# Four units of a projection sum in PSUM banks borrowed from the scan, and three weights' low parts move from POOL to VectorE

## The chip, the cores and the metric

The kernel runs on one core of one Trainium2 chip. The metric is the device time of one execution, in microseconds (us); the number given for a kernel is the median of its runs.

## The reference

One inference step of a two-layer encoder for 1024 new frames and 64 frames of a running stream, 1088 columns in all. Layer 0 mixes with a Mamba-2 scan (SSD), layer 1 with attention over a band of chunks; a gated feed-forward part follows each. The change lies in the entry of layer 0's mixer:

```python
zxbcdt = u @ w_in                       # u: rmsnorm of x, (1088, 1024)
z   = zxbcdt[..., :D_INNER]             # 2048 columns
xbc = zxbcdt[..., D_INNER:D_INNER + CONV_DIM]
dt_raw = zxbcdt[..., D_INNER + CONV_DIM:]
conv = conv_b
for k in range(CONV_W):                 # 4 taps
    conv = conv + padded[:, k:k + L] * conv_w[k]
xbc = silu(conv)                        # -> x (2048), B (4 x 128), C (4 x 128)
dt = softplus(dt_raw + dt_bias)
Acs = cumsum(dt * A)                    # within each chunk
y = scan(x, dt, Acs, B, C, state)       # decays exp(Acs_i - Acs_j), states from chunk to chunk
y = (y + x * D) * silu(z)
```

All arithmetic is float32. A matmul is made of three passes: each operand is split into a high part (rounded to the form that TensorE takes, float32r) and a low part (the rest), and high x high, high x low and low x high are summed.

## The kernel before, in words

Everything is held transposed, features on the 128 partitions and frames along the free axis, in three **slices** of 384, 384 and 320 columns (`SL`). The output features of `w_in` are taken in tiles of 128: x0 to x15, z0 to z15, four tiles each of B and C. A **unit** is one tile of one slice: 8 blocks of the contraction, 3 matmuls each, 24 in all (L417 to L419), summed in one PSUM bank, then evicted. Half a unit is 12 matmuls; after it the emitter may put other PE work in between (`st.pump()`).

**PSUM.** Eight banks: the pool `mm` has two (units), `ax` two (transposes and small products), `yy` four. `yy` serves three things one after the other: the entry's first units (tile `mmp`) and the products for dt (`dtp`); then the three transposed tables of Acs (`acT`, L683); then, for the rest of the mixer, the scan's outputs `yp` and `yo` (L864, L873). A pool hands its banks out in turn, and the next user of a bank waits for the last reader of the one before.

**Weights.** One tile of weights is loaded into `raw` (two buffers), then split by `part`: ACT casts the high part (L301) and another engine subtracts for the low part (L302) into `hl` (three buffers). That engine is `W.eng` where it is set, VectorE (DVE) otherwise. `W.eng` is POOL from just ahead of the entry's first units until the last of its nine, and in this stretch three weights are split: those of x1, z0 and x2, as B0's, C0's and x0's weights come free. Nothing else on POOL there is longer than 0.42 us.

**The entry.** First come B0, C0 and x0, three slices each. Then pairs follow by the list `order`; the first pair is x1 and z0, in the sequence x1 slice 0, z0 slice 0, x1 slice 1, z0 slice 1, x1 slice 2, z0 slice 2. Each x, B or C unit is evicted by DVE (L698, times the norm's factor; in two pieces for the third slice) into `craw` (three buffers), then convolved: ACT makes the first tap (L736) into `cvt` (a single buffer), DVE adds three (L738), ACT applies silu (L742, L744, L745) into the tile named by its kind: `BT`, `CT`, `xsT`. POOL copies the three halo columns between slices (L721, L726, L729). A z unit is evicted into `zs`.

Between these units PE also makes, for each slice of B0 and C0, the transposes `bnp` of BT (L762) and the products `cbp` of CT and BT (L768); and the table of dt is made: DVE steps L652 to L666 (a softplus by a series), products `acsp` (L669) and `lastp` (L674), the transposes `acT` (L683), DVE and ACT copies of them to `acr` (L684, L686), DMAs to DRAM (L685, L687), and from there the broadcast rows `dm` (L789) with which the scan's masks begin (L821, L825, L826). `dec` and `cd` (L688 to L690) are two further tables.

PE's order is that of the program text; the order on the other engines is set by the scheduler of the tile framework, from priorities and its own estimates.

Of the kernel before, what the change touches and what calls it, by code (L numbers as in the profile page):

```python
# [8 lines left out]
F32 = mybir.dt.float32  # L9
# [7 lines left out]
P = 128  # L17
# [6 lines left out]
SL = [(0, 384), (384, 384), (768, 320)]  # L24
# [14 lines left out]

GAP_A, GAP_B = 1.8, 1.2  # L40
HNP = 400
RB_WAIT = 4.8
CHW = ((13.1, 8.8, 18.0), (7.5, 6.0, 20.5)), ((9.0, 5.2, 18.0), (10.5, 8.0, 21.0))
AT_W1, AT_W2 = 6.0, 2.5
# [291 lines left out]
def hybrid_kernel(  # L336
# [5 lines left out]
    V, A, G, PE = nc.vector, nc.scalar, nc.gpsimd, nc.tensor  # L342
# [24 lines left out]
    for _ in range(17):  # L367
# [14 lines left out]
    W = Weights(  # L382
        nc, Ring(wp, "raw", RAWB, [P, 1024]), Ring(wp, "hl", HLB, [P, 2, 1024], F32R),
        Ring(None, "half", 0, [P, 2, 512], F32R), Ring(None, "tt", 0, [P, 1024]),
    )
# [16 lines left out]
    def mm(name):  # L402
        return pmm.tile([P, 512], F32, tag="mm", name=name)
# [5 lines left out]
    def passes(ps, w, rhs, ks, n, parts=2, first=True, last=True):  # L409

        h, v = w["w"]
        nk = len(ks)
        cut = (nk + parts - 1) // parts
        for i, (kw, k) in enumerate(ks):
            h_, l_ = h[:, kw * P:(kw + 1) * P], v[:, kw * P:(kw + 1) * P]
            xh, xl = rhs(k)
            PE.matmul(ps[:, :n], h_, xh, start=(first and i == 0), stop=False)  # L417
            PE.matmul(ps[:, :n], h_, xl, start=False, stop=False)  # L418
            PE.matmul(ps[:, :n], l_, xh, start=False, stop=(last and i == nk - 1))  # L419
            st.t += 3 * n / MMR  # L420
            if (i + 1) % cut == 0 and i + 1 < nk:
                st.pump()

    def unit(w, u, n, evac, parts=2, pl=None):
        ps_ = mm("mm") if pl is None else pl.tile([P, 512], F32, tag="mm", name="mmx")
        passes(ps_, w, lambda k: u[k], [(k, k) for k in range(KD)], n, parts=parts)
        evac(ps_)
        st.pump()
# [40 lines left out]
    def diag(r3, nb):  # L469
        dg = DG.get()  # L470
        V.tensor_tensor(
            dg[:, :nb], ident.unsqueeze(1).to_broadcast([P, nb, P]), r3.unsqueeze(2).to_broadcast([P, nb, P]), op=ALU.mult
        )
        return dg
# [11 lines left out]
    def rb_steps(ssum, n, out, wait=None, rb=None, more=None):  # L486
# [5 lines left out]
        with tc.high_priority(HIP):  # L492
            dg = diag(nr[:, :nb], nb)
        yield 0.1, wait or RB_WAIT
        with tc.high_priority(HIP):
# [15 lines left out]
    u, ucells = {}, {}  # L511
# [11 lines left out]
    order = []  # L523
# [47 lines left out]
    def project(qs, uq, y, src, after=None, early=None, pl=None):  # L571
# [3 lines left out]
        for mg in MGS:  # L575
            ws = early if early and mg is MGS[0] else [W.get() for _ in mg]
            for q in qs:
                n = QS[q][1]
                st.wait_for(lambda: q in uq)
                for m, w_ in zip(mg, ws):  # L580
                    ym = y[q][m // 4][:, m % 4, :]

                    def ev(ps):
                        with tc.high_priority(HIP):
                            if src is None:
                                A.copy(ym, ps[:, :n])
                            else:
                                V.tensor_tensor(ym, src[q][m // 4][:, m % 4, :], ps[:, :n], op=ALU.add)

                    if not (ws is early and q == qs[0]):  # L590
                        unit(w_, uq[q], n, ev, pl=pl)
                    if after:
                        if m == 0:
                            ss[q] = ssum_start(n)
                        add_sq(ss[q], ym, n, m == 0)
                    if q == qs[-1]:
                        W.put()
                if mg is MGS[-1]:
                    R.put(4)
                    if src is not None and src is not y:  # L600
                        R.put(2)
                    if after:
                        after(q, ss[q])

    with ExitStack() as es:
        pyy = es.enter_context(tc.tile_pool(reuse_waits="tile", name="pyy", bufs=4, space=PSUM))
# [172 lines left out]
        def ssd_task(j, s):  # L779
# [55 lines left out]
            for i in range(3):  # L835
# [5 lines left out]
                hn = sb2.tile([P, P], F32, tag="h", bufs=6, name="hn")  # L841
                with tc.high_priority(HNP if q < 2 else 0):
                    if c == 0:
# [61 lines left out]
        def evac_of(kind, i):  # L905
            if kind == "z":
                def f(s, p_):
                    n = SL[s][1]
                    zst[i, s] = sb2.tile([P, 384], F32, tag="zs", bufs=3, name="zs")
                    scaled(zst[i, s][:, :n], p_, s, 0, n)  # L910
                    A.activation(zst[i, s][:, :n], zst[i, s][:, :n], AF.Silu)
                    if i == 15:
                        drop_u(s)
                        if s == 0:
                            st.spawn(build_y())
                return f
            if kind == "x":
                cvx = pair_t[i] = Conv(i, "xsT", 6)

                def f(s, p_):  # L920
                    cvx(s, p_)
                    st.spawn(ssd_task(i, s), SSD_D + (1.5 if i and i % 4 == 0 and s == 0 else 0))
                return f
            if kind == "B":
                grp_t[i] = Conv(16 + i, "BT", 2), Conv(20 + i, "CT", 5)
                return grp_t[i][0]
            cvc = grp_t[i][1]

            def f(s, p_):
                cvc(s, p_)  # L930
                st.spawn(group_task(i, s), SSD_D)
            return f
# [53 lines left out]
        for s in range(NSL):  # L986
# [3 lines left out]
            if s == 0:  # L990
# [1 line left out]
                    A.copy(d_[:, :, 0:32], dtr3[:, 4 * i:4 * i + 4, :])  # L992
                    V.tensor_tensor(d_[:, :, 32:64], dtr3[:, 4 * i:4 * i + 4, :], d_[:, :, 0:32], op=ALU.subtract)
                A.activation(negA, pbs[:, 32:64], AF.Exp)
        W.eng = G
        first = [("B", 0), ("C", 0), ("x", 0)]
        ws = [W.get(), W.get()]
        ev = [evac_of(*f) for f in first]
# [13 lines left out]
        for s in range(NSL):  # L1012
            us, n = u[s], SL[s][1]
            pl, tg = pyy, "yy"
# [26 lines left out]
        for grp in order:  # L1041
            ws = [W.get() for _ in grp]
            ev = [evac_of(*f) for f in grp]
            if len(grp) < 3:
                seq = [(i, s) for s in range(NSL) for i in range(len(grp))]
            else:
                seq = [(0, 0), (1, 0), (0, 1), (0, 2), (2, 0), (1, 1), (2, 1), (1, 2), (2, 2)]
            for i, s in seq:
                kd_, jj_ = grp[i]
                q = 3 * jj_ + s  # L1050
                if kd_ == "x":
                    st.wait_for(lambda: so["C"] > q - 6)
                elif kd_ == "z":
                    st.wait_for(lambda: so["D"] > q - 3)
                elif kd_ == "C" and q >= 5:
                    g_, s_ = divmod(q - 5, 3)
                    st.wait_for(lambda: so["C"] > 3 * (4 * g_ + 3) + s_)
                unit(ws[i], u[s], SL[s][1], lambda p_: ev[i](s, p_))
                if s == 2:
                    W.put()  # L1060
        nc.sync.dma_start(cst_o, cst)
# [136 lines left out]
    def plain_pairs(ts, ops, hd, px, tmp):  # L1198

        n = ops.n  # L1200
        ws = [(W.get(), W.get()) for t_ in ts]
        for q in range(2):
            st.wait_for(lambda: all(a_ in ops.plain for a_ in (f"a{q + 1}1", f"a{q + 1}2")))
            uq = ops.plain[f"a{q + 1}1"] + ops.plain[f"a{q + 1}2"]
            for t_, w2 in zip(ts, ws):
                x = tmp.tile([P, n], F32, tag=("p1", "u3")[q] + f"{t_ % 2}", name="x")

                def gate(ps):
                    with tc.high_priority(HIP):
                        A.activation(x, ps[:, :n], AF.Silu)  # L1210

                def mult(ps):
                    with tc.high_priority(HIP):
                        V.tensor_tensor(x, ps[:, :n], x, op=ALU.mult)
                    nc.sync.dma_start(hd[:, t_, q * n:(q + 1) * n], x)

                for w, e in zip(w2, (gate, mult)):
                    unit(w, uq, n, e, pl=px)
                    if q:
                        W.put()  # L1220
# [248 lines left out]
    with ExitStack() as es:  # L1469
# [286 lines left out]
        for j in range(1, 8):  # L1756
# [3 lines left out]
            ws = [W.get(), W.get(), W.get() if j > 1 else wv]  # L1760
# [141 lines left out]
```

## Time and profile before

| | |
|---|---|
| runs | 3084.19, 3084.55, 3085.27 us; median 3084.55 |
| the profiled execution | 3085.35 us, of which 3083.7 from first to last instruction |
| busy over the span | PE 2972.3 us (96%), DVE 2120.9 (69%), ACT 1421.9 (46%), POOL 847.8 (27%) |
| granted TensorE clock, mean | 0.985 of full |

PE is busy nearly all the time, and so the stretches in which it is not are what to look at; the stage of the change is roughly 58 to 97 us of the span. Times of instructions are given from the span's start. A busy time on PE, a pipelined engine, overlaps with that of the next instruction; the distance between starts is what an instruction takes there.

### The profile page before, as it was taken

Reading aid. Unit: us, or ns where it says so; the run is one execution under the profiler, and the core shown is the slowest. Engines: PE = TensorE matmul, PEld = TensorE weight load, DVE = VectorE, ACT = ScalarE, POOL = GpSimd, SP = SyncE. Lnnn points to the kernel's source line nnn. Section 1 sums busy time; section 2 is a strip of 40 time slices with the busy share of each in tenths; the row PEclk is TensorE's granted clock in tenths of the full one; section 3 lists DMA queues with packets and bytes.
Section 4 is the critical chain, followed back from the end, with each engine's and each line's share of the span. In section 5 each row is a group of like instructions: output and inputs, shape, how many; then the busy total and the mean of one; then the engine's idle time right before and its main releaser. Section 6 shows DMA issues by size and latency. Waiting matters only on the chain. (4 is left out here: it accounts for less than half of the span.)

```text
span 3083.7 us, 57010 instructions
## 1 busy us (share of the span) xinstructions
PE 2972.3 (96%) x21665; PEld 2904.8 (94%) x21665; DVE 2120.9 (69%) x4579; ACT 1421.9 (46%) x2599; POOL 847.8 (27%) x972
## 2 busy tenths in 40 slices
PE   8999999999999999999999999999898999999998
PEld 7899999999999999999999889999898999999997
DVE  7888888885878545574566777777578645575544
ACT  5665656554543222344454655555553322244432
POOL 2334343421343334341231000000153334342112
PEclk9999999999999999999999999999999999999999
DMA  3333333335443222355563222222344222246664
GB/s 117 107 98 100 97 98 96 100 114 163 146 144 92 81 80 79 96 157 172 187 192 121 84 69 62 63 72 80 121 142 131 79 79 79 75 122 182 201 187 132
DMA packets 200419, 354.36 MB, mean 115 GB/s; under 512 B 21104, under 2 KB 150192, under 8 KB 200144
## 3 DMA queue, kind: packets, MB, share of 16 engines
q1 hardware_dynamic: 200080, 350.64, 37.3%
q8 instruction: 170, 2.79, 0.4%
q14 instruction: 105, 0.86, 0.1%
q0 software_dynamic: 64, 0.07, 0.0%
HBM read 283.30 MB, written 62.87 MB: 112 GB/s over the span
## 5 line engine op out<-in xcount | busy, mean ns | idle before, releaser
L417 PE MATMUL mm<-r,hl 128*128 128x384 f32 (+2 forms) x1664 | 561.1, 337 | 13.0 <-ACT r L1715 6.5
L302 DVE TENSOR_TENSOR hl<-raw,hl 128x1024 fp32r<-128x1024 f32 (+1 forms) x273 | 334.1, 1225 | 307.4 <-ACT hl L301 307.1
L419 PE MATMUL mm<-r,hl 128*128 128x384 f32 (+2 forms) x1664 | 542.0, 326 | 3.6 <-DVE hl L314 2.8
L418 PE MATMUL mm<-r,hl 128*128 128x384 f32 (+2 forms) x1664 | 541.1, 325 | 0.7 <-DVE r L1716 0.7
L301 ACT CAST hl<-raw 128x1024 fp32r<-128x1024 f32 (+1 forms) x276 | 279.1, 1012 | 276.1 <-DMA raw<-in_w_f_dram 99.5
L1239 PE MATMUL px<-r,hl 128*128 128x288 f32 (+1 forms) x1192 | 349.8, 293 | 0.0
L417 PEld LDWEIGHTS mm<-r,hl 128*128 128x128 f32 x1664 | 318.1, 191 | 15.2 <-ACT r L1715 6.7
L443 POOL TENSOR_TENSOR ssum<-ssum,sq 128x256 f32<-128x256 f32 (+3 forms) x153 | 171.0, 1120 | 572.2 <-ACT sq L442 568.7
L419 PEld LDWEIGHTS mm<-r,hl 128*128 128x128 f32 x1664 | 316.8, 190 | 5.1 <-DVE hl L314 4.0
L418 PEld LDWEIGHTS mm<-r,hl 128*128 128x128 f32 x1664 | 318.2, 191 | 1.4 <-DVE r L1716 1.0
L1238 PE MATMUL px<-r,hl 128*128 128x288 f32 x1056 | 311.6, 295 | 7.1 <-DVE u L1253 6.8
L1240 PE MATMUL px<-r,hl 128*128 128x288 f32 x1056 | 310.8, 294 | 0.0
L1240 PE MATMUL px<-rx,hl 128*128 128x256 f32 x816 | 228.7, 280 | 7.4 <-DVE hl L302 7.3
L1238 PE MATMUL px<-rx,hl 128*128 128x256 f32 x816 | 229.4, 281 | 0.1
L1239 PEld LDWEIGHTS px<-r,hl 128*128 128x128 f32 x1192 | 223.9, 188 | 0.1
L1409 PE MATMUL po<-rx,hl 128*128 128x384 f32 (+1 forms) x640 | 207.8, 325 | 0.0
L1238 PEld LDWEIGHTS px<-r,hl 128*128 128x128 f32 x1056 | 198.5, 188 | 9.1 <-DVE u L1253 8.5
L1408 PE MATMUL po<-rx,hl 128*128 128x384 f32 (+1 forms) x608 | 199.4, 328 | 0.0
L1240 PEld LDWEIGHTS px<-r,hl 128*128 128x128 f32 x1056 | 198.3, 188 | 0.0
L1410 PE MATMUL po<-rx,hl 128*128 128x384 f32 (+1 forms) x608 | 197.7, 325 | 0.5 <-DVE hl L302 0.5
L1239 PE MATMUL px<-rx,hl 128*128 128x256 f32 x680 | 190.3, 280 | 0.0
L259 POOL TENSOR_TENSOR tt<-raw 128x512 f32<-128x512 f32 x44 | 60.1, 1366 | 401.6 <-DMA raw<-in_w_f_dram 328.7
(336 smaller groups left out, 8128.9 us busy)
## 6 DMA issues: line engine op xcount, KB each, us to landing
raw<-in_w_f_dram SPq DMA_DIRECT2D x204, 512.0 KB, 3.7
raw<-in_w_in_dram SPq DMA_DIRECT2D x40, 512.0 KB, 3.8
raw<-in_w_f_dram SPq DMA_DIRECT2D x48, 384.0 KB, 3.2
sg<-hscr SPq DMA_DIRECT2D x88, 192.0 KB, 3.6
raw<-in_w_so_dram SPq DMA_DIRECT2D x32, 512.0 KB, 3.9
dm<-acd SPq DMA_DIRECT2D x64, 192.0 KB, 3.8
raw<-in_w_kv_dram SPq DMA_DIRECT2D x18, 512.0 KB, 3.7
raw<-in_w_o_dram SPq DMA_DIRECT2D x16, 512.0 KB, 3.7
```

The lines of the kernel that those rows point to most:

```text
L301: self.nc.scalar.copy(h, v)
L302: (eng or self.eng or self.nc.vector).tensor_tensor(lo, v, h, op=ALU.subtract)
L417: PE.matmul(ps[:, :n], h_, xh, start=(first and i == 0), stop=False)
L418: PE.matmul(ps[:, :n], h_, xl, start=False, stop=False)
L419: PE.matmul(ps[:, :n], l_, xh, start=False, stop=(last and i == nk - 1))
L443: (eng or G).tensor_tensor(ssum[:, :n], ssum[:, :n], q[:, :n], op=ALU.add)
L1238: PE.matmul(ps, wh, ah[:, k, :], start=(k == 0), stop=False)
L1239: PE.matmul(ps, wh, al[:, k, :], start=False, stop=False)
L1240: PE.matmul(ps, wl, ah[:, k, :], start=False, stop=(k == 3))
L1408: PE.matmul(ps[:, :n], wh, xh, start=(k == 0), stop=False)
L1409: PE.matmul(ps[:, :n], wh, xl, start=False, stop=False)
L1410: PE.matmul(ps[:, :n], wl, xh, start=False, stop=(k == FT - 1))
```

## The change

`unit` takes the tag of a pool as well as the pool. For the first pair of `order` the units x1 slice 0, z0 slice 0, x1 slice 1 and z0 slice 1 (`LENT`) take their bank from `yy`, not `mm`; their tiles are then named `mmx`. And `W.eng` is no longer set to POOL, so that the low parts of x1's, z0's and x2's weights are made by DVE. Lines after 41 are one higher in the changed kernel, those after 1058 two.

```diff
+LENT = (0, 0), (1, 0), (0, 1), (1, 1)
...
-    def unit(w, u, n, evac, parts=2, pl=None):
-        ps_ = mm("mm") if pl is None else pl.tile([P, 512], F32, tag="mm", name="mmx")
+    def unit(w, u, n, evac, parts=2, pl=None, tag="mm"):
+        ps_ = mm("mm") if pl is None else pl.tile([P, 512], F32, tag=tag, name="mmx")
...
-        W.eng = G
+        W.eng = None
...
-                unit(ws[i], u[s], SL[s][1], lambda p_: ev[i](s, p_))
+                lent = grp is order[0] and (i, s) in LENT
+                unit(ws[i], u[s], SL[s][1], lambda p_: ev[i](s, p_), pl=pyy if lent else None, tag="yy" if lent else "mm")
```

PE's order does not change. The four units take the four banks of `yy`, in turn those of slice 1's `dtp`, slice 1's `mmp`, slice 2's `dtp` and, after the tables, that of x1's second unit again; the tables `acT` take those of slice 2's `mmp`, of x1's first and of z0's first unit.

On DVE this stood in the middle of the dt table before (`rb_150` is the norm's factor of the third slice; `mm` here C0's unit):

```order
L698 TENSOR_TENSOR craw<-mmp,rb_150 128x64
L655 TENSOR_SCALAR tt<-tt 128x288
L656 RECIPROCAL tt<-tt 128x288
L698 TENSOR_TENSOR craw<-mm,rb_150 128x256
L657 TENSOR_TENSOR tt<-tt 128x288
L698 TENSOR_TENSOR craw<-mm,rb_150 128x64
L658 TENSOR_TENSOR tt<-tt 128x288
L738 SCALAR_TENSOR_TENSOR cvt<-craw,pcs,cvt 128x384
```

and this stands there now:

```order
L699 TENSOR_TENSOR craw<-mmp,rb_150 128x64
L303 TENSOR_TENSOR hl<-raw,hl 128x1024
L656 TENSOR_SCALAR tt<-tt 128x288
L657 RECIPROCAL tt<-tt 128x288
L699 TENSOR_TENSOR craw<-mm,rb_150 128x256
L658 TENSOR_TENSOR tt<-tt 128x288
L303 TENSOR_TENSOR hl<-raw,hl 128x1024
L659 TENSOR_TENSOR tt<-tt 128x288
L739 SCALAR_TENSOR_TENSOR cvt<-craw,pcs,cvt 128x384
```

Two low parts (L303) have come in, a third follows seven rows further down, and the second piece of C0's third slice has moved back, behind the multiply-adds of B0's.

A little later on DVE the evictions of x0's third slice and of x1's first have changed places with table steps. Before:

```order
L662 SCALAR_TENSOR_TENSOR dec<-dec,tt 128x288
L698 TENSOR_TENSOR craw<-mm,rb_148 128x384
L663 TENSOR_SCALAR dec<-dec 128x288
L738 SCALAR_TENSOR_TENSOR cvt<-craw,pcs,cvt 128x323
L664 SCALAR_TENSOR_TENSOR dt<-tt,dec 128x288
```

and now:

```order
L663 SCALAR_TENSOR_TENSOR dec<-dec,tt 128x288
L699 TENSOR_TENSOR craw<-mm,rb_150 128x256
L664 TENSOR_SCALAR dec<-dec 128x288
L739 SCALAR_TENSOR_TENSOR cvt<-craw,pcs,cvt 128x323
L665 SCALAR_TENSOR_TENSOR dt<-tt,dec 128x288
L739 SCALAR_TENSOR_TENSOR cvt<-craw,pcs,cvt 128x323
L666 MEMSET dt 64x32
L699 TENSOR_TENSOR craw<-mm,rb_150 128x64
L667 SCALAR_TENSOR_TENSOR tt<-dt,early 128x288
L739 SCALAR_TENSOR_TENSOR cvt<-craw,pcs,cvt 128x323
L699 TENSOR_TENSOR craw<-mmx,rb_148 128x384
```

Both pieces of x0's third slice now stand at the end of the table, and x1's first slice (`rb_148`) behind them and behind C0's last multiply-add. Beyond that ACT makes `acr` ahead of `cd`, one mask step (L822) of the scan's second slice stands ahead of a product of its first, and POOL's rows are the same without the three low parts, but for the places of a few copies. SP's order is the same.

## The prediction

> **What bounds the kernel now.** I read the windows first, to see which engine leads where. In each row stand the stretch, its length, busy time with instructions for PE, PEld, DVE, ACT and POOL, the granted TensorE clock, the DMA share and GB/s.
>
> ```profile
> span 3083.7 us, 57010 instructions
> ...
> 97.30:160.00 62.70, 55.66 (x391) 51.87 (x389) 62.45 (x159) 40.58 (x55) 27.38 (x36) 0.95 0.44 130
> 160.00:640.00 480.00, 478.94 (x3361) 464.60 (x3360) 414.41 (x1046) 282.23 (x408) 187.57 (x312) 1.00 0.34 99
> ```
>
> From 160 on PE has no room (478.94 of 480.00); from 97.3 to 160 DVE has none (62.45 of 62.70). Neither queue holds anything that stands at a fixed time, so what reaches 97 us earlier should end earlier by as much. The change lies before that, where the timeline of PE shows the one large hole. Columns: start, length, engine, line, operation, and in brackets the idle time before it with its releaser.
>
> ```profile
> 69.46 0.34 PE L419 MATMUL mm<-r,hl 128*128 128x384 f32 x1
> 75.72 0.66 PE L417 MATMUL mm<-r,hl 128*128 128x384 f32 x1 [5.92 <-ACT BT L745]
> ...
> 82.95 0.78 PE L768 MATMUL cbp<-CT,BT 128*128 128x128 f32 x6
> 83.53 0.42 PE L417 MATMUL mm<-r,hl 128*128 128x384 f32 x1
> ...
> 85.70 0.65 PE L669 MATMUL acsp<-tt,U 128*128 128x288 f32 x2
> ...
> 88.75 1.19 PE L683 MATMUL acT<-ident,acs 128*32 128x128 f32 x9
> ```
>
> The 5.92 us stand before the first slice of z0. Its bank is the one that x0's third slice filled, so it waits until DVE has evicted that slice. The releaser named is the activation that made BT, which ended near the same moment (75.66, in a row below). DVE's timeline shows the eviction (L698, in two pieces, at 72.16 and 75.36) and what stood before it:
>
> ```profile
> 60.46 0.86 DVE L655 TENSOR_SCALAR tt<-tt 128x288 f32<-128x288 f32 x1 [2.21 <-ACT tt L654]
> ...
> 63.51 0.44 DVE L657 TENSOR_TENSOR tt<-tt 128x288 f32<-128x288 f32 x1
> ...
> 64.00 2.66 DVE L658 TENSOR_TENSOR tt<-tt 128x288 f32<-128x288 f32 x1
> ...
> 67.12 2.48 DVE L659 TENSOR_SCALAR dec<-tt 128x288 f32<-128x288 f32 x1
> ...
> 72.16 0.41 DVE L698 TENSOR_TENSOR craw<-mm,rb 128x256 f32<-128x256 f32 x1
> ...
> 74.52 0.54 DVE L738 SCALAR_TENSOR_TENSOR cvt<-craw,pcs,cvt 128x323 f32<-128x323 f32 x1
> ...
> 75.36 0.21 DVE L698 TENSOR_TENSOR craw<-mm,rb 128x64 f32<-128x64 f32 x1
> ...
> 75.86 0.55 DVE L698 TENSOR_TENSOR craw<-mm,rb 128x384 f32<-128x384 f32 x1
> 76.33 0.29 DVE L663 TENSOR_SCALAR dec<-dec 128x288 f32<-128x288 f32 x1
> ...
> 78.10 0.55 DVE L738 SCALAR_TENSOR_TENSOR cvt<-craw,pcs,cvt 128x323 f32<-128x323 f32 x1
> 78.57 0.45 DVE L666 SCALAR_TENSOR_TENSOR tt<-dt,early 128x288 f32<-128x288 f32 x1
> ```
>
> Three rows are too long: L658 takes 2.66 where L657, of the same shape, takes 0.44; L659 and L655 take 2.48 and 0.86 where L663 takes 0.29. POOL's low parts lie over them and end with them:
>
> ```profile
> 58.76 2.40 POOL L302 TENSOR_TENSOR hl<-raw,hl 128x1024 fp32r<-128x1024 f32 x1 [0.73 <-ACT hl L301]
> ...
> 63.96 2.39 POOL L302 TENSOR_TENSOR hl<-raw,hl 128x1024 fp32r<-128x1024 f32 x1
> ...
> 66.67 2.76 POOL L302 TENSOR_TENSOR hl<-raw,hl 128x1024 fp32r<-128x1024 f32 x1
> ```
>
> L658 runs from 64.00 to 66.66, across the second and into the gap before the third; L659 ends at 69.60, the third at 69.43. So I read them as DVE held up by POOL: 2.22 + 2.19 + 0.57 = 4.98 us.
>
> The hole costs twice. The windows on the clock's own 3.41-us grid show it (the column after POOL):
>
> ```profile
> 71.17:74.58 3.41, 0.00 (x0) 0.00 (x0) 3.41 (x10) 1.43 (x3) 0.84 (x4) 1.00 0.30 118
> ...
> 77.99:81.41 3.42, 3.42 (x13) 3.33 (x13) 1.83 (x5) 1.22 (x3) 0.19 (x1) 0.50 0.01 2
> ...
> 2310.32:2313.73 3.41, 1.69 (x15) 1.49 (x14) 3.41 (x3) 1.98 (x3) 0.40 (x2) 1.00 0.68 252
> 2313.73:2317.14 3.41, 3.18 (x15) 3.18 (x16) 2.84 (x5) 1.05 (x1) 0.00 (x0) 0.50 0.00 0
> ...
> 2382.00:2385.41 3.41, 1.79 (x15) 1.79 (x16) 3.41 (x4) 2.75 (x4) 2.05 (x2) 1.00 0.17 57
> 2385.41:2388.82 3.41, 3.28 (x28) 3.07 (x27) 3.41 (x4) 1.20 (x2) 2.25 (x2) 1.00 0.21 58
> ```
>
> After a window without work PE ran at 0.50 until 81.41. The last four rows show where the line lies: after 1.69 us of work in 3.41 the clock fell, after 1.79 it did not.
>
> **Part 1, the banks.** No instruction is added; the PE order is the same, four units write other banks. z0's first slice then needs only its weights and a bank evicted long ago, so it starts 0.17 behind the row at 69.46, at 69.63 instead of 75.72: 6.09 us. Its weights are there: POOL began the low part of the second weight at 63.96, so its inputs were ready then.
>
> The half clock goes with the hole. From 75.72 to 83.53 (7.81 us) PE did two half units, three transposes and cbp. At full clock a half unit is 85.70 - 83.53 = 2.17, cbp 0.58 (82.95 to 83.53), the transposes about 0.2 (estimated from the half unit's columns): 5.1. That is 2.7 more, 8.8 together.
>
> The lent banks come due at acT, which takes the banks of x1's and z0's first slices, and at z0's second slice, which takes that of x1's second. The cover is DVE's lead: by the working below the first two are evicted about 5 us before acT. For the third the cover is short: its matmuls end just ahead of acT, whose 1.19 us (88.75) must hide an eviction of 0.55 (75.86), so 0.6 is left, and what DVE is later than that would be PE's.
>
> **Part 2, the low parts.** POOL loses three instructions (7.55 us), on an engine for which nothing here waits. DVE gains three:
>
> ```profile
> 102.27 1.21 DVE L302 TENSOR_TENSOR hl<-raw,hl 128x1024 fp32r<-128x1024 f32 x1
> 103.40 0.54 DVE L738 SCALAR_TENSOR_TENSOR cvt<-craw,pcs,cvt 128x323 f32<-128x323 f32 x1
> ...
> 75.42 0.24 ACT L745 ACTIVATE BT<-cvt 128x64 f32<-128x64 f32 x1
> ...
> 79.01 0.24 ACT L745 ACTIVATE CT<-cvt 128x64 f32<-128x64 f32 x1
> ```
>
> Each takes 1.13 (102.27 to 103.40). The first falls into DVE's 2.21 us of waiting before 60.46 and costs nothing. The other two lengthen DVE's queue by 2.26; the hold-up that goes gives back 4.98.
>
> **What is late next.** PE now reaches the transposes of BT (third slice) and then cbp before DVE and ACT have made their inputs. BT: the third multiply-add stood at 74.52; less 4.98, plus 2.26, less 0.41 for an eviction now behind it, 71.39; it ends 0.54 later, and BT 0.60 after that (75.06 to 75.66 in the rows), at 72.53. PE is there at 69.63 + 2.17 = 71.80: a wait of 0.7. Then transposes and half a unit: 74.90. CT: 78.10 - 4.98 + 2.26 - 0.10 (the step of 0.45 at 78.57 now ahead of it, the 0.55 eviction at 75.86 behind it) = 75.28, plus 0.55 and 0.60, 76.43: a wait of 1.5. cbp's 0.58 gives 77.01 for the start of x1's second slice, which was 83.53.
>
> The sum: -6.1 - 2.7 + 0.7 + 1.5 = **-6.5 us** (with rounding). Nothing from there to acT is changed.
>
> **What carries it.** acT starts the chain to the first mask rows:
>
> ```profile
> 91.16 0.42 ACT L689 ACTIVATE cd<-lastp 128x288 f32<-128x288 f32 x1
> ...
> 89.89 2.79 SPq L685 DMA_DIRECT2D acd<-acr  x3
> 92.77 1.30 SPq L687 DMA_DIRECT2D acd<-acr  x3
> 94.17 0.85 SPq L789 DMA_DIRECT2D dm<-acd  x2
> ...
> 96.26 1.06 SPq L789 DMA_DIRECT2D dm<-acd  x2
> ...
> 97.31 1.66 DVE L821 SCALAR_TENSOR_TENSOR dm<-dm,acs,mask 128x128 f32<-128x128 f32 x6 [2.40 <-DMA dm<-acd]
> ...
> DMA to landing us min/median/max: 3.1/4.1/4.5
> ```
>
> SP's queue is the same, so all of it moves with acT. Two edits change this chain. ACT makes acr before cd: a gain of 0 to 0.42, the latter if ACT, not SP, sets the pace. One mask step of the next slice now stands near 99.8 on DVE; its rows are issued at 96.26 and land 3.1 to 4.5 later, so (last row, from issue to landing of the mask rows between 93 and 112) DVE may wait 0 to 1.0 there, with the whole packed stage behind it. I take the two as cancelling.
>
> The clock has to hold through the two new waits. By the windows at 2310.32 and 2382.00 I ask for 1.8 us of work in each window. The longer wait takes 1.53 and has 2.37 of work ahead of it, which leaves 1.9: enough, narrowly.
>
> The Trainium skill, "TensorE: Matmul & The Clock Gate", section "HAM oscillation — how this bites in real kernels", asks only that no idle gap exceed about 3.4 us. By that rule the two waits are far from any danger and rival (b) below has no place; the row at 2310.32 contradicts it, since no gap of 3.4 us fits into a window with 1.69 us of work.
>
> The hold-up can turn round: POOL's halo copy for x0's third slice may now wait for the third low part on DVE, 1.21 at most. By the working above it is asked for some 4 us before that slice's eviction, so I cost it at nothing; without those 4 us it would be 1.21.
>
> The Trainium skill, "SBUF — State Buffer", section "Who interferes with whom", has one port pair that these two engines share, kept for a whole instruction by whichever starts first. By that rule the long rows are POOL's doing, rival (a) below has no place, and the 4.98 stands; the row at 64.00 agrees (2.66 against 0.44). That DVE also holds off POOL no row of before shows.
>
> **Rivals.** (a) *The hold-up isn't POOL's.* Then DVE pays 2.26 and gets nothing back: CT comes at 81.4, PE idles as long as before, a little later, and the half clock stays. x1's second slice starts near 82 plus up to 2: no change, 3084.5. Against it are three long rows that start and end with POOL's. 0.08. (b) *The clock drops again.* If the waits come 0.2 us longer, one window falls under half and the next does 1.71 us of work in 3.42: -4.8, so 3079.8. 0.15. (c) *More than I count.* The waits of 0.7 and 1.5 are shorter, since ACT or DVE runs ahead of my list: up to -8.7, 3075.9. 0.12. (d) *Slower.* Every later window shifts against the clock's grid. Many lie near half, as 2310.32 and 2382.00 show; each that falls costs 1.71. Four more eat the gain; eight give +7, 3091.7. But 6.5 is nearly two windows (6.83), so the pattern hardly moves against the grid. 0.04. That the change does not do what it says, the bank not being what PE waited for, is 0.02: the eviction ended at 75.57, the matmul began at 75.72.
>
> **The numbers.** The forecast has 0.59. The profiled execution took 3085.35, 1.65 outside its span; less 6.5, 3078.85. The median of the runs lies 0.8 under it: **3078.0**. Its own range is 3077.1 to 3079.5: the bounds on the chain (0.4 less, 1.0 more) and 0.5 either way for some ten spacings read from rows. To leave out no more than 2 in 10, the range reaches to (b) and (c): 3075.5 to 3081.5. A measurement of this kernel tells 0.2%, 6.2 us, from no change, and the forecast stands just beyond that: 0.42 of its 0.59 and nearly all of (c) are faster, 0.53; (a), (b) and the rest are the same, 0.43; slower 0.04.
>
> **What would show it.** Right: z0's first slice follows x1's without a gap; L658 and L659 take 0.4 and 0.3; two PE waits, near 72 and 75, of 0.7 and 1.5; no window at 0.50 before 97; acT near 82.2, the first mask step near 90.8. Wrong: L658 still over 2 us, a wait of PE at z0's second slice for its bank, a half-clock window in 71 to 82, or an acT that is 6.5 early with an end that is not.

## The result, and the profile after

The changed kernel takes 3077.34 us (median of 19 runs, 3070.98 to 3082.62), the kernel before 3082.77 (19 runs, 3078.14 to 3086.26). The ratio is 0.9983, 95% interval 0.9977 to 0.9990: 3.1 to 7.1 us less, 5.2 in the middle. The profiled execution took 3078.88, its span 3077.2.

PE's timeline of the changed kernel, at the places shown of before:

```profile
68.80 0.33 PE L420 MATMUL mmx<-r,hl 128*128 128x384 f32 x1
68.97 0.33 PE L418 MATMUL mmx<-r,hl 128*128 128x384 f32 x1
...
71.78 0.55 PE L763 MATMUL bnp<-ident,BT 128*128 128x128 f32 x3 [0.56 <-ACT BT L745]
...
75.77 0.88 PE L769 MATMUL cbp<-CT,BT 128*128 128x128 f32 x6 [1.36 <-ACT CT L745]
76.46 0.42 PE L418 MATMUL mmx<-r,hl 128*128 128x384 f32 x1
...
81.68 1.20 PE L684 MATMUL acT<-ident,acs 128*32 128x128 f32 x9
```

z0's first slice (68.97) now starts 0.17 us behind the last matmul of x1's first; the 5.92 us are gone, and in their place stand two waits, for BT and for CT. DVE's timeline shows where those come from:

```profile
58.05 1.23 DVE L303 TENSOR_TENSOR hl<-raw,hl 128x1024 fp32r<-128x1024 f32 x1 [0.46 <-ACT hl L302]
59.80 0.31 DVE L656 TENSOR_SCALAR tt<-tt 128x288 f32<-128x288 f32 x1 [0.53 <-ACT tt L655]
...
62.66 1.22 DVE L303 TENSOR_TENSOR hl<-raw,hl 128x1024 fp32r<-128x1024 f32 x1
63.80 0.45 DVE L659 TENSOR_TENSOR tt<-tt 128x288 f32<-128x288 f32 x1
...
64.69 0.30 DVE L660 TENSOR_SCALAR dec<-tt 128x288 f32<-128x288 f32 x1
...
66.71 1.22 DVE L303 TENSOR_TENSOR hl<-raw,hl 128x1024 fp32r<-128x1024 f32 x1
...
74.72 0.55 DVE L739 SCALAR_TENSOR_TENSOR cvt<-craw,pcs,cvt 128x323 f32<-128x323 f32 x1
...
89.49 1.66 DVE L822 SCALAR_TENSOR_TENSOR dm<-dm,acs,mask 128x128 f32<-128x128 f32 x6 [1.65 <-DMA dm<-acd]
...
92.00 0.34 DVE L822 SCALAR_TENSOR_TENSOR dm<-dm,acs,mask 128x128 f32<-128x128 f32 x1
```

The three long rows are short: 0.31, 0.45 and 0.30 where 0.86, 2.66 and 2.48 stood. Three low parts (L303) are new; the first lies in what was a wait of 2.21 us, of which 0.46 and 0.53 are left. CT's third multiply-add is at 74.72. The first mask step is at 89.49 (97.31 before), and the one that was moved (92.00) waits for nothing. The windows around the old hole, in the columns and at the times of before, stand at full clock:

```profile
71.17:74.58 3.41, 2.68 (x16) 2.31 (x15) 3.32 (x12) 1.22 (x3) 0.73 (x4) 1.00 0.00 0
74.58:77.99 3.41, 2.22 (x15) 2.22 (x16) 3.34 (x8) 2.07 (x5) 0.65 (x3) 1.00 0.01 2
77.99:81.41 3.42, 3.42 (x20) 3.29 (x19) 2.37 (x5) 1.28 (x3) 0.19 (x1) 1.00 0.07 22
```

This execution's own clock grid lies elsewhere (a window of it starts at 97.47, see the last section, and so one at 73.58). On it the window that holds the wait of 1.36 has 2.05 us of work, more than the 1.8 that the prediction asked for.

### The profile page after: what moved, and what is told of

Read it like the earlier page. It is cut to its first block, busy times and chain, and to the rows that moved or that the text cites. A ratio compares the mean times of both kernels' runs of the same rounds, so it can differ in the third digit from the quotient of the medians.

```text
span 3077.2 us, 57007 instructions
## 1 busy us (share of the span) xinstructions
PE 2974.8 (97%) x21665; PEld 2908.0 (95%) x21665; DVE 2120.1 (69%) x4582; ACT 1422.8 (46%) x2599; POOL 844.3 (27%) x969
## 3 DMA queue, kind: packets, MB, share of 16 engines
q8 instruction: 170, 2.79, 0.4%
## 5 line engine op out<-in xcount | busy, mean ns | idle before, releaser
L418 PE MATMUL mm<-r,hl 128*128 128x384 f32 (+2 forms) x1632 | 549.0, 336 | 7.0 <-ACT r L1717 6.3
L303 DVE TENSOR_TENSOR hl<-raw,hl 128x1024 fp32r<-128x1024 f32 (+1 forms) x276 | 337.5, 1224 | 307.3 <-ACT hl L302 306.2
L420 PE MATMUL mm<-r,hl 128*128 128x384 f32 (+2 forms) x1632 | 530.5, 325 | 3.6 <-DVE hl L315 2.8
L419 PE MATMUL mm<-r,hl 128*128 128x384 f32 (+2 forms) x1632 | 529.7, 325 | 0.7 <-DVE r L1718 0.7
L418 PEld LDWEIGHTS mm<-r,hl 128*128 128x128 f32 x1632 | 311.7, 191 | 8.9 <-ACT r L1717 6.5
L420 PEld LDWEIGHTS mm<-r,hl 128*128 128x128 f32 x1632 | 310.4, 190 | 5.3 <-DVE hl L315 4.2
L419 PEld LDWEIGHTS mm<-r,hl 128*128 128x128 f32 x1632 | 311.6, 191 | 1.4 <-DVE r L1718 1.0
```

What stands on the lines that cost most here:

```text
L303: (eng or self.eng or self.nc.vector).tensor_tensor(lo, v, h, op=ALU.subtract)
```

## Experiments: which part does what

**How they are measured.** A single execution of one kernel may differ by several us from the next (3071 to 3083 above), so the totals tell little apart; the stage in the trace tells more. Even there the start varies: in some executions the clock is at half for a window near 22 us or near 57 us, and then all that follows is later. I therefore count from the start of the first transposes `bnp` (64.47 before, 63.81 after; on PE the same work lies ahead of them in all kernels) to three points: the start of `acT`, the second store of the scan's output y, and one load of weights that SP issues at 243.18 before and 235.43 after, in the stretch where PE has no room. The expectations below say "from the first transposes" or, in the first four, "by the clock of the third mmp eviction", which is 6.77 to 7.11 earlier.

| kernel | ratio to before, 95% | first transposes | to acT | to y's 2nd store | to the load | from there to the span's end |
|---|---|---|---|---|---|---|
| before | | 64.47 | 24.28 | 56.62 | 178.71 | 2840.5 |
| before, second profile | | 63.38 | 22.94 | 55.39 | 177.48 | 2833.2 |
| after | 0.9983 (0.9977 to 0.9990) | 63.81 | 17.87 | 49.46 | 171.62 | 2841.8 |
| after, again | 0.9982 (0.9973 to 0.9991) | 66.66 | 17.37 | 49.84 | 171.97 | 2837.6 |
| lending alone | 1.0000 (0.9991 to 1.0008) | 63.87 | 21.43 | 55.42 | 178.53 | 2835.3 |
| low parts alone | 1.0010 (1.0001 to 1.0019) | 66.67 | 25.83 | 58.89 | 181.20 | 2834.6 |
| POOL writes only | 0.9984 (0.9975 to 0.9993) | 64.02 | 16.72 | 49.37 | 171.48 | 2838.0 |
| the same, with lending | 0.9985 (0.9976 to 0.9994) | 65.52 | 16.53 | 50.43 | 175.23 | 2839.0 |
| low parts twice | 0.9990 (0.9981 to 0.9999) | 66.66 | 21.00 | 53.47 | 175.58 | 2837.6 |
| third low part on POOL | 0.9990 (0.9981 to 0.9999) | 64.30 | 19.34 | 51.92 | 174.04 | 2831.1 |
| third low part later | 0.9988 (0.9979 to 0.9996) | 65.37 | 17.23 | 51.19 | 173.32 | 2832.5 |
| group work later | 0.9980 (0.9971 to 0.9989) | 65.34 | 14.82 | 48.90 | 173.57 | 2834.6 |
| both of these | 0.9987 (0.9978 to 0.9996) | 65.35 | 14.82 | 49.04 | 172.13 | 2834.4 |

All ratios rest on 10 runs or more of the kernel, and the second profile of before is a single run; in the three later sets the kernel before stood at 3080.7, 3080.9 and 3080.3. My theory was that of the prediction: PE waited for a bank that DVE, held up by POOL's low parts, gave back late, and after the change PE waits for DVE's own row of work.

**The lending alone.** The low parts stay with POOL:

```diff
-        W.eng = None
+        W.eng = G
```

> The lending alone; the three low parts stay on POOL. Times are told from the start of the third x0 slice's mmp eviction on DVE (57.69 before, 57.03 after), since what lies ahead of it is the same in all kernels; by that clock the acT product starts at +31.1 before and at +24.7 after. Theory (both halves are needed): z0's first slice follows x1's first without a gap and no window near it is at half clock, but the three long DVE rows stay (2.7, 2.5, 0.9 us), so BT's transposes keep TensorE waiting some 3.9 us and cbp some 1.2 us; acT at about +27.5, +29.5 if the clock drops in those waits; total 1 to 3.6 us below before. Rival (the lending brings it all, the low parts nothing): acT at +24.7 as after, total 6 us below before.

DVE's timeline has the long rows of before, and PE's has the wait at BT:

```profile
63.41 2.66 DVE L659 TENSOR_TENSOR tt<-tt 128x288 f32<-128x288 f32 x1
...
66.52 2.49 DVE L660 TENSOR_SCALAR dec<-tt 128x288 f32<-128x288 f32 x1
```

```profile
74.97 0.90 PE L763 MATMUL bnp<-ident,BT 128*128 128x128 f32 x3 [3.69 <-ACT BT L745]
...
79.39 0.88 PE L769 MATMUL cbp<-CT,BT 128*128 128x128 f32 x6 [0.48 <-ACT CT L745]
```

3.69 us where 3.9 were expected; one window at half clock follows (the transposes take 0.90, not 0.55), so CT's wait is 0.48, not 1.2. acT is 2.85 us nearer to the first transposes than before. The rival, that lending brings it all, falls. But of the 2.85 only 0.2 is left at the load near 243 (both against the first profile of before; against the second, which also has one such window, 1.5 nearer at acT and some 1 us later at the load), and the total does not move: the expected 1 to 3.6 us did not come. Where they went is shown further down.

**The low parts alone.** The kernel before, nothing lent:

```diff
-        W.eng = G
+        W.eng = None
```

> The low parts on VectorE alone; nothing is lent. Theory: the three long DVE rows fall to 0.4, 0.3 and 0.3 us, but DVE's order then has x0's third-slice eviction behind more steps, so z0's first slice still waits for its bank: it starts 1 to 3 us earlier than before by the clock of the third mmp eviction (+18.0 before), with a gap of 3 to 5 us ahead of it and a stretch at half clock; acT at +28 to +30; total 1 to 3 us below before. Rival (POOL's low parts were all of it): gap under 1 us, acT at +25 or earlier. Rival (POOL does not hold DVE up): the three rows stay long, acT +33.

This one missed on the side that matters: it is slower, by 0.3 to 5.9 us in the total, and acT comes 1.5 to 2.9 later than in the two profiles of before. PE's row, then two of DVE's, then one of DVE's of before:

```profile
66.67 0.49 PE L762 MATMUL bnp<-ident,BT 128*128 128x128 f32 x3
74.44 0.66 PE L417 MATMUL mm<-r,hl 128*128 128x384 f32 x1 [7.28 <-ACT BT L745]
```

```profile
66.32 0.45 DVE L658 TENSOR_TENSOR tt<-tt 128x288 f32<-128x288 f32 x1
...
74.07 0.22 DVE L698 TENSOR_TENSOR craw<-mm,rb 128x64 f32<-128x64 f32 x1
```

```profile
63.87 0.22 DVE L698 TENSOR_TENSOR craw<-mm,rb 128x64 f32<-128x64 f32 x1
```

DVE is no longer held up (0.45). But the hole, 7.28, has moved ahead of x1's first slice: that slice takes the bank of C0's third slice, whose second piece of eviction (64 columns) DVE's new order has at 74.07; before it stood at 63.87. Behind the hole PE's clock is at half until 80.56. I had looked at x0's eviction alone. So the move of the low parts brings an order that needs the lending, and neither part gains by itself.

**POOL writes but does not read.** The kernel before, DVE's order untouched; the low parts of three weights are left out of the products and replaced by two memsets each:

```diff
-            (eng or self.eng or self.nc.vector).tensor_tensor(lo, v, h, op=ALU.subtract)
+            if self.eng is not None and eng is None:
+                self.eng.memset(lo.bitcast(F32), 0.0)
+                self.eng.memset(lo.bitcast(F32), 0.0)
+            else:
+                (eng or self.nc.vector).tensor_tensor(lo, v, h, op=ALU.subtract)
```

> The kernel before, with each of POOL's low parts of x1, z0 and x2's first weights replaced by two memsets of the same tile on POOL: POOL writes as much, but reads nothing; the low parts of those weights are left out of the product. Everything else, DVE's order too, is that of before. Theory (a POOL subtraction that reads two SBUF tiles holds off DVE's): the three DVE rows fall to 0.4, 0.3 and 0.3 us, x0's third-slice eviction comes 5 us earlier, the gap ahead of z0's first slice falls from 5.9 to about 0.9 us, no half clock after it; acT at +23.4 to +24 (before: +31.1); total 7 us below before. Rival (any work of POOL's holds DVE up, or the rows are long by themselves): the rows stay at 2.7 and 2.5 us where they meet the memsets, acT at +30 to +31, total as before.

DVE, POOL and PE:

```profile
63.00 0.45 DVE L662 TENSOR_TENSOR tt<-tt 128x288 f32<-128x288 f32 x1
...
63.94 0.30 DVE L663 TENSOR_SCALAR dec<-tt 128x288 f32<-128x288 f32 x1
...
64.68 0.46 DVE L665 SCALAR_TENSOR_TENSOR dec<-dec,tt 128x288 f32<-128x288 f32 x1
...
69.99 0.23 DVE L702 TENSOR_TENSOR craw<-mm,rb 128x64 f32<-128x64 f32 x1
```

```profile
64.24 0.95 POOL L303 MEMSET hl<- 128x1024 f32 x1 [0.74 <-PE mm L423]
```

```profile
70.36 0.41 PE L421 MATMUL mm<-r,hl 128*128 128x384 f32 x1 [1.02 <-ACT BT L749]
```

The rows are short, a step with two inputs that runs under a memset (64.68) keeps its length, x0's eviction comes at 69.99, and the hole is 1.02. acT is 23.5 us behind the third mmp eviction, in the expected 23.4 to 24. At the load near 243 this is 7.2 us ahead of the first profile of before, as much as the whole change brings. So the hold-up by POOL is the cause of the hole, and the bank is only where PE met it. (The memsets end before L662 and L663; that those rows would be short under a longer write is not shown.)

**Lending as well.** The memsets of the last diff, in the kernel with the lending alone:

```diff
-        W.eng = None
+        W.eng = G
```

> The lending, with POOL's low parts of x1, z0 and x2 replaced by two memsets each (these low parts are left out of the products). Times from the first transposes bnp. Theory (what kept the bank was DVE's delay behind POOL; once that is gone the lending has only the last 1.0 us of PE's gap to remove): no gap at z0's first slice, no wait at BT or cbp, acT at +15.5 to +15.9 (memsets without lending +16.72, after +17.87, before +24.28). But DVE's order has mask steps set apart among convolution steps here, as in the four kernels that lost 1.8 to 2.3 us between the first mask rows and 42 us after the first transposes; if that order is what costs, this kernel loses as much there and at 243 us stands no earlier than the memsets without lending (-7.2 against before). Rival (the earlier acT comes through): at 243 us it stands 8.2 to 8.6 before.

```profile
76.14 0.88 PE L773 MATMUL cbp<-CT,BT 128*128 128x128 f32 x6 [0.80 <-ACT CT L749]
```

BT is waited for no more, cbp waits 0.80 (none was expected), and acT is at 16.53, only 0.19 nearer than with the memsets alone (15.5 to 15.9 was expected). At the load it stands 3.5 us before the first profile of before, not 7.2; what lies between, the row of mask steps, is taken up below. The totals of the two kernels with memsets cannot be told apart (0.9984 and 0.9985).

**Low parts twice.** The changed kernel with each of the three subtractions done twice on DVE.

```diff
             (eng or self.eng or self.nc.vector).tensor_tensor(lo, v, h, op=ALU.subtract)
+            if self.dbl:
+                self.nc.vector.tensor_tensor(lo, v, h, op=ALU.subtract)
...
-        W.eng = None
+        W.dbl = True
...
-                    W.eng = None
+                    W.dbl = False
```

> The changed kernel with each of the three low parts computed twice in a row on VectorE, 3 x 1.2 us more of DVE's time ahead of BT and CT. Theory (after the change DVE's row of work is what TensorE waits for): the first doubling partly fills waits (about 1 us of them), the other two come through whole; the waits of BT's transposes and cbp grow from 0.56 and 1.36 us together by 2.3 to 3 us, acT at +27 to +27.7 by the clock of the third mmp eviction (after: +24.7), 1.7 more if the clock drops; total 2.3 to 4.5 us above the changed kernel, 1 to 4 below before. Rival (DVE has slack there, TensorE's own row sets the time): acT stays at +24.7, total as the changed kernel.

```profile
77.66 0.90 PE L765 MATMUL bnp<-ident,BT 128*128 128x128 f32 x3 [3.56 <-ACT BT L747]
```

The wait for BT grows by 3.0, one window at half clock follows, and cbp does not wait behind that. acT is at 21.00: 3.1 and 3.6 later than in the two profiles of after. DVE's row does set PE's time there.

**The third low part, back on POOL or later.** First the changed kernel with POOL named again ahead of the third alone:

```diff
+                if s == 2 and i == 2:
+                    W.eng = G
                 if s == 2:
                     W.put()
```

> The changed kernel, with the third low part alone given back to POOL. DVE loses 1.13 us of its own work and meets one POOL subtraction of 2.4 us. Theory (a POOL instruction that reads SBUF holds off DVE's two-input ones until it ends): one DVE row near 66 to 68 grows by 1.9 to 2.3 us, so DVE's row is 0.8 to 1.2 us later in sum, the waits of BT's transposes and cbp grow by that, acT at +18.7 to +19.1 from the first transposes (after: +17.87). Rival (DVE isn't held up): no long row, acT at +16.7 to +17.

```profile
66.31 2.74 DVE L739 SCALAR_TENSOR_TENSOR cvt<-craw,pcs,cvt 128x384 f32<-128x384 f32 x1
```

```profile
65.64 2.98 POOL L303 TENSOR_TENSOR hl<-raw,hl 128x1024 fp32r<-128x1024 f32 x1 [2.36 <-ACT hl L302]
```

The same multiply-add took 0.61 in the row before it: 2.1 us of hold-up for 1.13 saved. acT is at 19.34, 1.5 to 2.0 later; 0.8 to 1.2 were expected. Then the low part asked for after x1's second slice:

```diff
-                if s == 2:
+                if s == 2 and i < 2:
                     W.put()
...
+                if grp is order[0] and (i, s) == (0, 1):
+                    W.put()
```

> The changed kernel, with the third low part (x2's weight) asked for only after x1's second slice, so that on DVE it comes behind the third slices of B0 and C0 instead of ahead of them: DVE's 1.13 us leave the row that BT and CT wait in. Times from the first transposes bnp (64.47 before, 63.81 after); acT starts at +24.28 before and +17.87 after. Theory (DVE's row sets PE's two waits): the wait of BT's transposes (0.56) goes, that of cbp falls from 1.36 to 0.8, acT at +16.7; total 1.1 us below the changed kernel, 6.5 below before. POOL's halo copy (1.76 us after) takes 0.2 again. Rival (the low parts on DVE cost nothing there, or ACT sets the waits): acT stays at +17.9.

```profile
76.67 0.88 PE L769 MATMUL cbp<-CT,BT 128*128 128x128 f32 x6 [1.48 <-ACT CT L745]
```

BT's wait goes, cbp's becomes 1.48 instead of 0.8: the scheduler set x1's eviction ahead of CT's last multiply-add, and that gave part of the 1.13 back. acT is at 17.23, 0.1 to 0.6 nearer, and the total (0.9988) shows no gain over the changed kernel.

**Group work later.** PE's order is changed so that units stand where it waited, alone and with the third low part later:

```diff
-                st.spawn(group_task(i, s), SSD_D)
+                st.spawn(group_task(i, s), SSD_D + (2.2 if i == 0 and s == 2 else 0))
```

> The changed kernel, with PE's group work of the third slice put later in PE's order: BT's transposes behind acsp, cbp behind acT, so that units stand where PE waited. Theory (PE waits for BT and CT, and nothing else is late there): both waits (0.56 and 1.36) go and cbp's 0.7 us move behind acT, so acT comes at +15.3 to +16 from the first transposes bnp (after: +17.87), the first mask step 1.9 to 2.6 earlier than after; total 1.9 to 2.6 us below the changed kernel, 7.5 below before. Rival (DVE's table step for acsp, or SP's chain, is late next): PE's wait moves to acsp or acT, acT at +17 to +18, total as the changed kernel.

> Both edits: the third low part behind x1's second slice, and the third slice's group work later in PE's order. Theory: PE has no wait left between the first transposes and acT, so this gives what the later group work alone gives (acT at +15.3 to +16), and the 1.13 us of DVE are worth nothing more; total 1.9 to 2.6 us below the changed kernel. Rival (DVE sets acT even then, through the table step that acsp waits for): another 1.1 us earlier than the later group work alone.

Both waits go, and acT is at 14.82 in both, so PE's row, not DVE's, sets it then. That is 2.5 to 3 us better than after. Yet at the load these two stand at 173.57 and 172.13, behind after's 171.62 and 171.97. In the total they cannot be told from the changed kernel.

**Where a nearer acT goes.** From acT to y's second store the table gives 31.6 and 32.5 us for after, 32.3 and 32.5 for before, 32.5 to 33.1 for the low parts alone, twice, on POOL or replaced by memsets without lending; but 33.9 to 34.2 for the five others: lending alone, lending with memsets, the third later, and both kernels with later group work. DVE's timeline of the kernel with later group work shows the order of rows; what the five have in common follows it:

```profile
86.44 0.56 DVE L699 TENSOR_TENSOR zs<-mmx,rb 128x384 f32<-128x384 f32 x1 [2.20 <-PE mmx L420]
88.03 0.62 DVE L739 SCALAR_TENSOR_TENSOR cvt<-craw,pcs,cvt 128x384 f32<-128x384 f32 x1 [1.04 <-ACT cvt L737]
88.57 0.34 DVE L822 SCALAR_TENSOR_TENSOR dm<-dm,acs,mask 128x128 f32<-128x128 f32 x1
88.83 0.61 DVE L739 SCALAR_TENSOR_TENSOR cvt<-craw,pcs,cvt 128x384 f32<-128x384 f32 x1
89.36 0.34 DVE L822 SCALAR_TENSOR_TENSOR dm<-dm,acs,mask 128x128 f32<-128x128 f32 x1
...
150.62 1.03 DVE L827 TENSOR_TENSOR dm<-dm,CB 128x384 f32<-128x384 f32 x2 [1.59 <-ACT dm L826]
```

After does six mask steps in one row (89.49, x6), with the convolution of x1's second slice ahead of them and ahead of the eviction of z0's second slice. Here the scheduler has put that eviction first, where it waits 2.20 us for PE, and of the three convolution steps behind it one stands just ahead of the mask steps and two between them; the other four kernels have steps of that convolution between the mask steps too. So the first product with CB (L827) starts 4.7 to 5.8 us behind the first mask step in these five, 2.5 to 2.9 in the other eight profiles. The stage behind is one in which DVE had no room before (62.45 of 62.70 us), so that little of what is lost here can be made up there. From that store to the load it is 122.1 to 122.3 us in all kernels but four of these five: 123.1 for lending alone and for both edits, 124.7 and 124.8 for later group work and for lending with memsets. The last row, a wait of 1.59 for ACT's exponentials that after does not have, stands there in the two longest (1.67 in the other). That the order is the cause is argued from five kernels against the rest, not shown: a kernel with this order and nothing else changed was not made.

**Second profiles.** Both kernels once more, without an edit:

> The kernel before once more, for a second profile. If the stage numbers belong to the program and not to one execution, acT starts 24.28 us after the first transposes bnp and the gap ahead of z0's first slice is 5.9 us again, within 0.3, or half a clock window (1.7 us) apart where the clock's grid falls otherwise; the stretch from 243 us to the end (2837.5 us in the first profile) may differ by several us.

> The changed kernel once more, for a second profile and five more rounds. If the stage numbers belong to the program: acT 17.87 us after the first transposes, waits of 0.56 and 1.36, no half clock between; 7.1 us earlier than before at 243 us (counted from the first transposes), all within 0.3 or half a clock window; the rest from there to the end (2838.75 in the first profile) anywhere from 2828 to 2839. Total 5 to 6 us below before.

PE of before, and its windows; then PE of after:

```profile
74.63 0.66 PE L417 MATMUL mm<-r,hl 128*128 128x384 f32 x1 [5.92 <-ACT BT L745]
...
86.32 1.20 PE L683 MATMUL acT<-ident,acs 128*32 128x128 f32 x9
```

```profile
70.59:74.01 3.42, 0.00 (x0) 0.00 (x0) 3.42 (x10) 1.02 (x2) 0.35 (x1) 1.00 0.17 71
74.01:77.42 3.41, 2.79 (x9) 2.82 (x10) 3.31 (x10) 1.22 (x3) 0.65 (x3) 0.50 0.00 0
77.42:80.83 3.41, 3.41 (x23) 3.37 (x22) 1.65 (x5) 1.22 (x3) 0.19 (x1) 1.00 0.01 2
```

```profile
78.10 0.88 PE L769 MATMUL cbp<-CT,BT 128*128 128x128 f32 x6 [1.34 <-ACT CT L745]
...
84.03 1.20 PE L684 MATMUL acT<-ident,acs 128*32 128x128 f32 x9
```

The hole is 5.92 again and cbp's wait 1.34. But before now has one window at half clock behind the hole, not two, and acT is 1.34 nearer; the windows of the first profile show why:

```profile
74.58:77.99 3.41, 2.27 (x7) 2.30 (x8) 3.35 (x11) 1.22 (x3) 0.65 (x3) 0.50 0.00 0
```

There the hole reached 1.14 us into the window and left 2.27 us of work, and the next one stayed at half; in the second it reached 0.62 in, left 2.79, and the next was at full. In after's second profile BT is not waited for, and acT is 0.5 nearer to the first transposes. That is PE, not DVE: its clock was at half from about 57 to 60 us, so its first transposes came 7.29 us behind the third mmp eviction instead of 6.78, and counted from that eviction acT is at 24.65 and 24.66 in the two profiles.

So the change brings 6.4 us at acT between the first profiles, 5.6 between the second, 7.1 and 5.5 at the load. From the load to the end the thirteen profiles differ by 10.7 us (2831.1 to 2841.8), with no relation to the edit that I can see, so one execution's total says little. Over the runs it does hold that what is early at the load is early at the end: against the mean of before's two profiles the eleven other rows lie from 3.1 us later (low parts alone) to 6.6 earlier (POOL writes only) at the load, and each lies inside the 95% interval of its total, which is some 5 us wide.

## Why the prediction was right, point by point

- **The hole.** Forecast: gone with the bank, -6.1. It is gone, in both traces of after. What made it is shown by the memsets: POOL's reading subtractions. Rival (a), that the hold-up is not POOL's, is out.
- **The half clock.** Forecast: -2.7. True of the execution that was read, where two windows fell. In the other only one did, and acT came 1.34 sooner. The term was sized from one phase of the clock's grid; 1.3 to 2.7 would have been its bounds, and this is the term that the second pair of profiles makes smaller (5.6 at acT).
- **DVE's sum.** Forecast: 4.98 returned, 2.26 added, the first low part free. The rows are 0.31, 0.45, 0.30 and the first low part lies in the old wait.
- **The new waits.** Forecast 0.7 and 1.5, measured 0.56 and 1.36 (none and 1.34 in the second profile). Counted between starts the two cost a little more, 2.3 together: from 68.97 to 76.46 are 7.49 us, and the same work without a wait takes 5.16 in the kernel with memsets alone (70.36 to 75.52), close to the prediction's 5.1. The clock held, so rival (b) did not come; nor did (c), since the waits are as long as forecast within 0.2.
- **acT.** Forecast 6.5 earlier; from the first transposes 6.41 (5.57 between the second profiles). The lent banks cost nothing: x1's second slice is evicted from 81.67 to 82.22, inside acT (81.68 to 82.88), and PE waits for no bank.
- **The chain.** Forecast: two edits that cancel. The moved mask step waits for nothing, so its up to 1.0 us did not come. The first mask step is 7.16 earlier (from the first transposes), 0.75 more than acT, because the first three stores of acr by SP, 2.79 us before, take 1.27. But that belongs to the one execution: in the second profile of before they take 1.28, and between the second profiles the first mask step gains 5.4, no more than acT. So neither edit of this chain shows a gain or a loss. SP of after, and of before's second profile:

```profile
82.78 1.27 SPq L686 DMA_DIRECT2D acd<-acr  x3
```

```profile
87.46 1.28 SPq L685 DMA_DIRECT2D acd<-acr  x3
```

- **The hold-up turned round.** It happened, at no cost, as put down, but for longer than the 1.21 allowed: POOL's halo copy waits over DVE's third low part and a step with two inputs on either side of it.

```profile
66.58 1.76 POOL L722 COPY craw<-halo 128x3 f32<-128x3 f32 x1 [3.79 <-DVE cvt L739]
```

  With the third low part later the copy at this place takes 0.26. The prediction says that no row of before shows this direction; its third POOL row may: it takes 2.76 where the others take 2.40 and 2.39, and a two-input step of DVE (66.59 to 67.19) was running when it began.

- **The end.** Forecast 3078.0, measured 3077.34. That the two lie so close is partly luck: the three runs of before that were shown had a median 1.8 above that of all 19, and the gain was 5.2, not 6.5, in the totals. The mechanism was right and its size a little high, by the half clock. By the prediction's own measure (a change under 6.2 us counts as none) the 5.2 are "the same", to which it gave 0.43, and not "faster", to which it gave 0.53; the 19 runs resolved more than it allowed for, since their interval of 3.1 to 7.1 us does not reach zero. Rival (d), a slower end through later windows, is not borne out by the mean; it is how single runs differ.
- **One sentence of the prediction does not hold in general**: that what reaches 97 us earlier ends earlier by as much. For this change it held (7.16 at the first mask step, 7.09 at the load). In five kernels of the study the way from acT to the load is 156.1 to 158.8 us, where the two kernels themselves have 153.8 to 154.6: 1.5 us or more of a nearer acT was lost on that way.

The Trainium skill, "SBUF — State Buffer", section "Who interferes with whom", says that a DVE instruction with two SBUF inputs contends with a POOL instruction that reads SBUF, and not with one that only writes. The traces agree for steps with two inputs: 2.66 and 2.74 under a subtraction, 0.46 under a memset. The long rows L655 and L659 have one input, which that sentence does not cover; they take 0.86 and 2.48 under the subtractions and 0.31 and 0.30 without, and none ran under a memset.

## What to carry to other kernels

An instruction that takes several times as long as its twin may be waiting for something that two engines share: look which engine's row ends with it, before moving banks or buffers. Where a scheduler sets the order, an edit that takes work on to an engine also moves other steps of that engine, so read the order of every eviction that gives back a bank, not only of the one in the hole. And follow a gain past the first point that it reaches: here several better starts were in part lost again behind acT, where DVE had no room.

## What the runs showed of the hardware that was not expected

- **POOL's small copies wait long.** With the low parts twice on DVE, a halo copy of 128x3 took 4.77 us:

```profile
69.46 4.77 POOL L724 COPY craw<-halo 128x3 f32<-128x3 f32 x1 [5.38 <-DVE cvt L741]
```

  It ran on through DVE's subtractions and the steps with two inputs between them and ended (74.23) just after DVE began a copy out of PSUM (74.10, Bn). In after the copy of 66.58 ended 0.13 after such a copy began as well (68.34 and 68.21). So in these rows DVE's two-input steps, one right behind the other, kept POOL out until the row ended, not for one instruction only.
- **The clock falls without a long gap.** In after, near 100 us, PE had two gaps, of 1.03 and 1.34, in one window, and the next was at half:

```profile
97.47:100.88 3.41, 1.04 (x7) 0.79 (x7) 3.41 (x10) 2.09 (x4) 0.83 (x1) 1.00 0.84 300
100.88:104.29 3.41, 3.41 (x15) 3.41 (x15) 3.41 (x13) 0.68 (x2) 0.00 (x0) 0.51 0.25 102
```

  1.04 us of work in 3.41, with no gap over 1.34. The rule quoted in the prediction from the Trainium skill ("TensorE: Matmul & The Clock Gate", section "HAM oscillation — how this bites in real kernels"), that no gap may exceed about 3.4 us, would let this pass; the trace does not agree. The grid of these windows lies elsewhere in each execution (75.72 fell 1.14 us into one, 74.63 in the other profile 0.62), and that alone moved acT by 1.34 us in an unchanged kernel. How long the half clock lasts behind a hole went with the work that PE did in the window in which the hole ended: with 2.27 us of it (before) and 2.71 (low parts alone) the next window stayed at half, with 2.79 (before's second profile), 2.86 (lending alone) and 2.87 (low parts twice) it was at full.
